# Quiet ends of the residuals and undisturbed reading of scores in a two-layer decoder trunk

## The chip, the cores and the metric

The kernel runs on one core of a Trainium2 chip. The metric is the device time of one execution in microseconds (us); a kernel's time is the median of its runs. The engines are TensorE (PE in the profile, PEld for its weight loads), VectorE (DVE), ScalarE (ACT), GpSimd (POOL) and SyncE (SP), which issues the transfers of the weights.

## The reference

One sequence of 256 tokens, width 1024, goes through two layers. Each layer has a half-step SwiGLU FFN, an attention, and another half-step FFN. Each of these sublayers is normalised first, shifted and scaled by vectors that are made from c, and gated by a third one:

```python
mod = silu(c) @ ada_w[layer] + ada_b[layer]
sh1, sc1, g1, sh2, sc2, g2, sh3, sc3, g3 = split(mod, 9)
h = rms_norm(x, norm_g[layer, 0]) * (1 + sc1) + sh1
x = x + 0.5 * g1 * swiglu(h, ffn_w_in[layer, 0], ffn_w_out[layer, 0])
h = rms_norm(x, norm_g[layer, 1]) * (1 + sc2) + sh2
x = x + g2 * mix        # layer 0: differential attention, layer 1: forgetting attention
h = rms_norm(x, norm_g[layer, 2]) * (1 + sc3) + sh3
x = x + 0.5 * g3 * swiglu(h, ffn_w_in[layer, 1], ffn_w_out[layer, 1])
```

In the differential attention each of 8 heads has two softmaxes over scores with a relative bias; the second, times lambda, is subtracted from the first, and the result multiplies v. All is in fp32.

## The kernel before, in words

**The matrices.** x lies transposed in SBUF, 8 tiles of 128 features by 256 tokens. Every product in fp32 is made of three matmuls on rounded halves (`mm3`): weight high times activation high, weight low times activation high, weight high times activation low. Weights come by SP in pieces of up to 128 x 1024 (`raw`, six buffers). ACT makes the high half of a piece (`wh`, a cast, `cp_part`), DVE the low half (`wl`, a subtraction, `sub_part`). For the normalised x the halves are `HH` and `HL`.

**The modulation.** The vectors sh, sc and g are made on DVE, out of the way of PE: one block (`ada`, 128 x 1024, `ada_block`, line 198) multiplies 128 rows of the weights by silu(c) and sums. Two blocks share a tile of 1 MB with three buffers; when the second one is done, its buffer is free and SP is told to load the next tile into it (`ada_dma`, line 185). There are 160 blocks. `need` (line 236) makes, at the place where it is called, all blocks that a modulation still lacks.

**What sets the order.** The program is written in one order, and a wrapper for each engine (`InOrder`, line 40) keeps a rough clock of its own for that engine. Casts, subtractions and ada blocks are background work: `bg` (line 386) issues them after each `mm3` where ACT's or DVE's clock is behind PE's; `fill_act` and `fill_dve` (lines 367 and 372) issue them ahead of an instruction whose operands are not ready by that clock. An ada block needs a credit, which grows with PE's work and is at most 6. `plain` and `plainly` run a function with the filling switched off. `take` (line 338) hands out the next weights of the stream and makes the halves that are still missing on the spot. `later` puts an operation off by some calls of `run_laters`.

**The residual.** `x_update` (line 438) adds gate times the product to one of the 8 tiles of x (DVE), writes the scaled tile's halves (HH on ACT, HL on DVE) and its square `sq` (ACT), and adds the squares up in `acc` (DVE behind an FFN, POOL behind an attention, the eighth always on DVE). The next sublayer starts on halves that are not normalised yet (`lp`, `lq`, or `lg` and `lu` of an FFN of kind "late"): PE runs its first steps, then the sum of `acc` over partitions (`psn`), from which `rstd_of` (line 460) makes the factor that is applied to the results. After its "late" first block an FFN goes on with halves that are normalised (`pg`, `pu`; `hid` is its hidden layer, `po` its output).

**The first attention.** A group for head t (line 1161) has the scores of head t, the transposed weights of t - 1, the values of t - 2, and the turned output of t - 3. `exps` (line 1084) reads the scores from PSUM on DVE in four instructions (`nl`, `nm`), each followed by an exponential on ACT. Groups 0 to 7 stand among the projections of v, q and k; 7 to 10 among the steps of the output projection (`pw`). Before the change, `exps` is plain in the group of the last head alone. `finish` (line 872) ends the output projection: it calls `need` for the attention's gate and for the scale and shift of the FFN behind it, which is 64 blocks from the start of the kernel, then updates x tile by tile.

**The start.** c is spread over all partitions by two matmuls (`pc`) of a row of ones with c in row 96 of a tile `crow`, whose other rows are zero; ACT makes silu(c) of it (`cact`). Before, between and behind, PE multiplies a constant tile (`warm`).

Of the kernel before, what the change touches and what calls it, by code (L numbers as in the profile page):

```python
# [10 lines left out]
F32 = mybir.dt.float32  # L11
F32R = mybir.dt.float32r
BF16 = mybir.dt.bfloat16
AF = mybir.ActivationFunctionType
ALU = mybir.AluOpType
PSUM = bass.MemoryType.PSUM

P = 128
D = 1024
S = 256  # L20
NC = D // P
HD = 64
AH = 8
# [17 lines left out]
CP_FIT = 0.9  # L41
DVE_FIT = 0.6
# [62 lines left out]
def trunk(ctx, tc, a, out):  # L105
# [3 lines left out]
    act = InOrder(tc, nc.scalar, 0.13, 1 / 1200)  # L109
    dve = InOrder(tc, nc.vector, 0.08, 1 / 960)  # L110
# [5 lines left out]
    kp = ctx.enter_context(tc.tile_pool(name="kp", bufs=2))  # L116
# [8 lines left out]
    def abank(name):  # L125
        return pp.tile([P, 512], F32, tag="ta", name=name)
# [6 lines left out]
    def plain(f, *args):  # L133

        r = []
        act.plainly(lambda: dve.plainly(lambda: r.append(f(*args))))
        return r[0]

    crow = ap_.tile([P, 2, D], F32, tag="ada", name="crow").rearrange("p a b -> p (a b)")
# [6 lines left out]
    ones = cp_.tile([P, P], F32, name="ones")  # L146
    first_in = []
    dve.memset(ones, 1.0 / D)
    dve.memset(crow[96:97, D:D + P], 1.0)
    dve.memset(crow[:96, :D + P], 0.0)  # L150
    eps = cp_.tile([P, 1], F32, name="eps")
    dve.memset(eps, EPS)
    half = cp_.tile([P, 2], F32, name="half")
# [136 lines left out]
    credit = [0.0]  # L290
    pace = [0.0]
    mode = ["hold"]
    laters = []

    def w_dma(count=NRAW):
# [65 lines left out]
    def work(cols):  # L361

        credit[0] = min(CREDIT, credit[0] + pace[0] * 2 * cols / 2048)
        if mode[0] != "hold":
            bg()

    def fill_act(start):
        while (mode[0] != "hold" and act.t + CP_FIT < start
               and len(his) < min(len(pieces), len(raws), done[0] + NHI)):
            cp_part()  # L370

    def fill_dve(start):

        while mode[0] != "hold" and dve.t + DVE_FIT < start:
            full = len(los) - begun[0]
            if mode[0] == "run" and credit[0] >= 1.0 and (full >= FULL or not splittable()):
                credit[0] -= 1.0
                dve.plainly(ada_block)
            elif splittable():
                sub_part()  # L380
            else:
                break
# [30 lines left out]
    def flush():  # L413
        for e in laters[:]:
            laters.remove(e)
            e[1]()

    def mm3(ps, w, xx, first, last):
        (wh, wl), (xh, xl) = w, xx
        mm(ps, wh, xh, start=first, stop=False, skip_group_check=True)  # L420
        mm(ps, wl, xh, start=False, stop=False, skip_group_check=True)
        mm(ps, wh, xl, start=False, stop=last, skip_group_check=True)
        work(P)
# [14 lines left out]
    def x_update(n, ps, gate, nxt, acc_eng):  # L438

        dve.scalar_tensor_tensor(x[n], ps, gate[:, n:n + 1], x[n], op0=ALU.mult, op1=ALU.add)
        hh, hl = hn[n]
        A = mods[nxt[0]][1]
        act.activation(hh, x[n], AF.Copy, scale=A[:, n:n + 1])
        sq = kp.tile([P, S], F32, tag="sq", name=f"sq{n}")
        act.activation(sq, x[n], AF.Square)

        def second():
            dve.scalar_tensor_tensor(hl, x[n], A[:, n:n + 1], hh.bitcast(F32),  # L450
                                     op0=ALU.mult, op1=ALU.subtract)
            if n == 0:
                acc[0] = sq
            else:
                t = kp.tile([P, S], F32, tag="acc", name="acc", bufs=1) if n == 1 else acc[0]
                (acc_eng if n < NC - 1 else dve).tensor_tensor(t, acc[0], sq, op=ALU.add)
                acc[0] = t
        return second

    def rstd_of(then=None, parts=None):  # L460
# [106 lines left out]
    def ffn(l, i, kind, m, nxt, at=2):  # L567
# [130 lines left out]
        for n in range(NC):  # L698
            po = mmbank(f"po{n}")[:, :S]
            if n == NC - NFILL:  # L700
                mode[0] = "fill"
            for hf in range(2):
                blk = take("wout")
                if n == NC - 1 and hf:
                    need(*nxt)
                    shift_cols(nxt)
                for kk in range(11):
                    k = hf * 11 + kk
                    if n == 0 and k == 18:
                        flush()  # L710
                        flush()
                    hh, hl = hid[k // 2]
                    o = (k % 2) * 256
                    mm3(po, blk(kk * P), (hh[:, o:o + 256], hl[:, o:o + 256]), k == 0, k == 21)
                    if kk in (1, 4, 6, 9):
                        run_laters()
            need(gate)
            if n >= 4:
                need(nxt[0])

            def upd(n=n, po=po):
                f = x_update(n, po, mods[gate][1], nxt, dve)
                if (l, i) == (0, 0) and n < NC - 1:
                    late["spread"](n)
                later(1, f)
            if n < NC - 1:
                later(1, upd)
            else:
                flush()
                flush()  # L730
                upd()
                flush()

    class Last:

# [194 lines left out]
    def warm(n):  # L930

        pw = bbank("warm")
        for _ in range(n):
            mm(pw[:, :P], ones, ones, start=True, stop=True)
# [21 lines left out]
    pc = [sbank(f"pc{i}") for i in range(2)]  # L956
    for i in range(2):
        mm(pc[i], crow[:97, D:D + P], crow[:97, i * 512:(i + 1) * 512], start=True, stop=True)
    psn = abank("psn")
    for k in range(0, NC, 2):  # L960
        sq = kp.tile([P, 512], F32, tag="w512a" if k % 4 else "w512b", name=f"sqs{k}")
        xk = xx[:, k:k + 2].rearrange("p a b -> p (a b)")
        if k == 2:
            dve.tensor_tensor(sq, xk, xk, op=ALU.mult)
        else:
            act.activation(sq, xk, AF.Square)
        sq4.append(sq)
        if k % 4:
            i = k // 4
            act.activation(cact[:, i * 512:(i + 1) * 512], pc[i], AF.Silu)  # L970
            sq = sq4[2 * i]
            dve.tensor_tensor(sq, sq, sq4[2 * i + 1], op=ALU.add)
            dve.tensor_tensor(sq[:, :S], sq[:, :S], sq[:, S:], op=ALU.add)
            warm(4 - 3 * i)
            for t in range(2):
                mm(psn[:, t:t + 1], sq[:, t * P:t * P + P], ones[:, :1], start=i + t == 0, stop=i == 1,
                   skip_group_check=True)
# [72 lines left out]
    def attention_a():  # L1050
# [33 lines left out]
        def exps(hd, sb):  # L1084
            g = gs[hd]
            nl = []
            nm = kp.tile([P, 4], F32, tag="nm", name=f"nm{hd}")
            sm = kp.tile([P, 4], F32, tag="sm", name=f"sm{hd}")
            for m in range(2):
                s = sb[m]  # L1090
                n_ = cp_.tile([P, 384], F32, tag=f"hidh{4 + 2 * (hd % 2) + m}", name=f"nl{hd}_{m}")
                nl.append(n_)
                for qt, (c0, w) in enumerate(QT):
                    cc = 2 * m + qt
                    dve.tensor_tensor_reduce(
                        n_[:, c0:c0 + w], s[:, c0:c0 + w], g[:, S - w:], -0.125, BIG,
                        ALU.add, ALU.min, accum_out=nm[:, cc:cc + 1])
                    act.activation(n_[:, c0:c0 + w], n_[:, c0:c0 + w], AF.Exp,
                                   bias=nm[:, cc:cc + 1], scale=-1.0,
                                   accum_out=sm[:, cc:cc + 1])  # L1100
            st[hd], sms[hd] = nl, sm
# [59 lines left out]
        def group(t):  # L1161

            hs, hw, hv, ho = (h if 0 <= h < AH else None for h in (t, t - 1, t - 2, t - 3))
            bank = bbank(f"po{t}") if hv is not None or ho is not None else None
            sb = scores(hs) if hs is not None else None
            pw = weights_t(hw) if hw is not None else None
            if hv is not None:
                values(hv, bank[:, :256])
            if ho is not None:
                out_t(ho, bank[:, 256:])  # L1170
            if hw is not None:
                wt = cp_.tile([P, 384], F32, tag=f"hidh{8 + hw % 2}", name=f"wt{hw}")
                act.copy(wt, pw[:, :384])
                st[hw] = wt
            if hs is not None:
                plain(exps, hs, sb) if hs == AH - 1 else exps(hs, sb)
            if hv is not None:
                squares(hv, bank[:, :256])
                inv_rms(hv)
            if ho is not None:  # L1180
                plain(out_split, ho, bank[:, 256:]) if ho == AH - 1 else out_split(ho, bank[:, 256:])
# [398 lines left out]
```

## Time and profile before

| what | before |
|---|---|
| median of 3 runs, us | 966.03 (965.13 to 966.9) |
| the profiled execution's own time, us | 964.94 |
| its span, us | 962.9 |
| instructions | 20487 |
| mean granted TensorE clock | 0.998 |
| moved by the transfers | 267.89 MB, mean 278 GB/s |

The prediction quotes rows of several views. A row of the timeline has start and duration in us from the span's start, the engine, the operation as out<-in with its shape, how many in a row it stands for, and in brackets the idle time of the engine ahead of it with what ended it. A row of the chain has start, duration, engine and tile. A row of the waits has who waited for whom, the total in us, how often, and the longest. A row of the windows has a stretch, its length, each engine's busy time with the count of its instructions, then TensorE's granted clock, the share of the DMA engines and GB/s. Names are those of the kernel without numbers; most instructions carry line 100, the wrapper's, so they are told by tile.

### The profile page before, as it was taken

How to read it: one execution, taken by the hardware profiler on the slowest of the kernel's cores; microseconds unless marked ns; L12 is line 12 of the kernel's file. 1: busy time of each engine (PE TensorE's matmuls, PEld its weight loads, DVE VectorE, ACT ScalarE, POOL GpSimd, SP SyncE). 2: the span in 40 equal slices, each digit the busy share in tenths (PEclk: the TensorE clock that was granted, in tenths of full speed). 3: DMA queues.
4: the chain of work that ended last, by engine and by line, in shares of the span. 5: the costliest groups of instructions: out<-in, count | busy, mean ns of one | idle time of the engine just before them, and what ended most of it. 6: DMA issues, size and time to landing. Idle time of an engine off the chain costs nothing.

```text
span 962.9 us, 20487 instructions
## 1 busy us (share of the span) xinstructions
PE 954.6 (99%) x8090; PEld 930.9 (97%) x8090; DVE 821.1 (85%) x1369; ACT 556.9 (58%) x908; POOL 72.5 (8%) x119
## 2 busy tenths in 40 slices
PE   9999999999999999999999999999999999999997
PEld 7999999988999999999997999999998899999997
DVE  8989988889999999878889988889988799555575
ACT  6575655566777645455577554445568766554432
POOL 0000001100112000000000000000044014200000
PEclk9999999999999999999999999999999999999999
DMA  9998989968767699878959899988995437987641
GB/s 369 413 368 311 376 314 317 372 216 292 280 214 255 211 389 375 293 280 315 330 198 369 303 340 339 343 294 317 317 323 163 118 128 219 268 166 253 192 148 44
DMA packets 69661, 267.89 MB, mean 278 GB/s; under 512 B 9572, under 2 KB 10413, under 8 KB 59454
## 3 DMA queue, kind: packets, MB, share of 16 engines
q1 hardware_dynamic: 66060, 259.35, 76.7%
q0 software_dynamic: 3072, 6.92, 2.5%
q8 instruction: 63, 1.03, 0.4%
q10 hardware_dynamic: 434, 0.33, 0.1%
q14 instruction: 32, 0.26, 0.1%
HBM read 264.42 MB, written 2.66 MB: 277 GB/s over the span
## 4 chain that ended last, share of the span: by engine, by line
PE 92%; DVE 4%; ACT 2%; issue 2%; DMA 0%; POOL 0%; SPq 0%; DVEq 0%; ACTq 0%; POOLq 0%
PE po L100 25%; PE pg L100 22%; PE pu L100 21%; PE pv L100 5%; PE pf L100 5%; PE lp L100 4%; PE pw L100 3%; DVE wl L100 1%; PE lq L100 1%; PE lu L100 1%; PE lg L100 1%; PE pk L100 1%; DVE nl L100 1%; PE wb L100 1%; ACT nl L100 1%
## 5 line engine op out<-in xcount | busy, mean ns | idle before, releaser
L100 ACT CAST wh<-raw 128x1024 fp32r<-128x1024 f32 (+1 forms) x360 | 347.8, 975 | 212.2 <-PE pu L100 87.2
L100 DVE TENSOR_TENSOR wl<-raw,wh 128x1024 fp32r<-128x1024 f32 (+1 forms) x360 | 400.1, 1126 | 76.1 <-ACT sg L100 25.0
L100 DVE CUSTOM_DVE_ANT_0 ada<-ada,cact,vecs 128x1024 f32<-128x1024 f32 x144 | 182.6, 1277 | 0.0
L100 PE MATMUL pg<-HH,wl 128*128 128x256 f32 x608 | 167.9, 276 | 0.0
L100 PE MATMUL pu<-HH,wh 128*128 128x256 f32 x608 | 167.9, 276 | 0.0
L100 PE MATMUL pg<-HH,wh 128*128 128x256 f32 x608 | 167.9, 276 | 0.0
L100 PE MATMUL pu<-HL,wh 128*128 128x256 f32 x608 | 167.9, 276 | 0.0
L100 PE MATMUL pg<-HL,wh 128*128 128x256 f32 x608 | 167.9, 276 | 0.0
L100 PE MATMUL pu<-HH,wl 128*128 128x256 f32 x608 | 167.9, 276 | 0.0
L100 PE MATMUL po<-hidh,wh 128*128 128x256 f32 x528 | 145.7, 276 | 0.0
L100 PE MATMUL po<-hidh,wl 128*128 128x256 f32 x528 | 145.7, 276 | 0.0
L100 PE MATMUL po<-hidl,wh 128*128 128x256 f32 x528 | 145.7, 276 | 0.0
L100 PEld LDWEIGHTS pg<-HH,wl 128*128 128x128 f32 x608 | 114.1, 188 | 0.0
L100 PEld LDWEIGHTS pg<-HH,wh 128*128 128x128 f32 x608 | 114.1, 188 | 0.0
L100 PEld LDWEIGHTS pg<-HL,wh 128*128 128x128 f32 x608 | 114.2, 188 | 0.0
L100 PEld LDWEIGHTS pu<-HH,wh 128*128 128x128 f32 x608 | 114.2, 188 | 0.0
L100 PEld LDWEIGHTS pu<-HL,wh 128*128 128x128 f32 x608 | 114.1, 188 | 0.0
L100 PEld LDWEIGHTS pu<-HH,wl 128*128 128x128 f32 x608 | 114.1, 188 | 0.0
L100 PEld LDWEIGHTS po<-hidl,wh 128*128 128x128 f32 x528 | 99.1, 188 | 0.0
L100 PEld LDWEIGHTS po<-hidh,wl 128*128 128x128 f32 x528 | 99.1, 188 | 0.0
L100 PEld LDWEIGHTS po<-hidh,wh 128*128 128x128 f32 x528 | 99.1, 188 | 0.0
L100 ACT CAST hidh<-hf 128x512 fp32r<-128x512 f32 x44 | 27.3, 621 | 45.4 <-DVE hf L100 45.4
(244 smaller groups left out, 1878.0 us busy)
## 6 DMA issues: line engine op xcount, KB each, us to landing
raw<-in_win SPq DMA_DIRECT2D x176, 512.0 KB, 5.8
ada<-in_ada SPq DMA_DIRECT2D x79, 1024.0 KB, 7.3
raw<-in_wout SPq DMA_DIRECT2D x48, 384.0 KB, 5.5
raw<-in_wout SPq DMA_DIRECT2D x48, 320.0 KB, 5.2
raw<-in_wqk SPq DMA_DIRECT2D x16, 512.0 KB, 5.2
raw<-in_wo SPq DMA_DIRECT2D x16, 512.0 KB, 5.2
raw<-in_wlast SPq DMA_DIRECT2D x16, 512.0 KB, 4.3
raw<-in_wv SPq DMA_DIRECT2D x8, 512.0 KB, 9.0
```

The lines of the kernel that those rows point to most:

```text
L100: return self.tc.keep_in_program_order(f(*args, **kw))
```

## The change

In the program's order of work four things change. While a flag `quiet` is set, no background work is issued; it is set in the last of the 8 output tiles of an FFN, after step 3 of its second half, and cleared when that tile of x is updated. In the last tile of any residual, `sq` is made ahead of HH, and `acc` ahead of HL. In the first attention `exps` is plain in all groups. At the start the large memset of `crow` stands ahead of the small one, one `warm` stands between the two matmuls that spread c, and two behind them are gone (four are three, one is none).

```diff
@@ start
     dve.memset(ones, 1.0 / D)
+    dve.memset(crow[:96, :D + P], 0.0)
     dve.memset(crow[96:97, D:D + P], 1.0)
-    dve.memset(crow[:96, :D + P], 0.0)
@@ work, fill_act, fill_dve
-        if mode[0] != "hold":
+        if mode[0] != "hold" and not quiet[0]:
             bg()
-        while (mode[0] != "hold" and act.t + CP_FIT < start
+        while (not quiet[0] and mode[0] != "hold" and act.t + CP_FIT < start
-        while mode[0] != "hold" and dve.t + DVE_FIT < start:
+        while not quiet[0] and mode[0] != "hold" and dve.t + DVE_FIT < start:
@@ x_update
+        sq = kp.tile([P, S], F32, tag="sq", name=f"sq{n}")
+        if n == NC - 1:
+            act.activation(sq, x[n], AF.Square)
         act.activation(hh, x[n], AF.Copy, scale=A[:, n:n + 1])
-        sq = kp.tile([P, S], F32, tag="sq", name=f"sq{n}")
-        act.activation(sq, x[n], AF.Square)
-
-        def second():
+        if n < NC - 1:
+            act.activation(sq, x[n], AF.Square)
+
+        def low():
             dve.scalar_tensor_tensor(hl, x[n], A[:, n:n + 1], hh.bitcast(F32),
                                      op0=ALU.mult, op1=ALU.subtract)
+
+        def second():
+            if n < NC - 1:
+                low()
...
                 (acc_eng if n < NC - 1 else dve).tensor_tensor(t, acc[0], sq, op=ALU.add)
                 acc[0] = t
+            if n == NC - 1:
+                low()
@@ ffn, output tiles
                     mm3(po, blk(kk * P), (hh[:, o:o + 256], hl[:, o:o + 256]), k == 0, k == 21)
+                    if n == NC - 1 and hf and kk == 3:
+                        quiet[0] = True
...
                 upd()
                 flush()
+                quiet[0] = False
@@ spread of c
         mm(pc[i], crow[:97, D:D + P], crow[:97, i * 512:(i + 1) * 512], start=True, stop=True)
+        warm(1 - i)
...
-            warm(4 - 3 * i)
+            if not i:
+                warm(3)
@@ group of the first attention
-                plain(exps, hs, sb) if hs == AH - 1 else exps(hs, sb)
+                plain(exps, hs, sb)
```

PE's order is the same but for the `warm` matmuls. On DVE, background work moves. The first place is the fifth head's group in the first attention, on DVE: `wl` is background subtractions, `nl` and `nm` the readings of the scores, `ada` a modulation block, `ss` the start of the norm of another head. Before:

```order
L100 TENSOR_TENSOR wl_3319<-raw_3018,wh_3206 128x1024
L100 ISA nl4_0_3351,nm4_3349<-s4_0_3332,g4_3169 128x128
L100 TENSOR_TENSOR wl_3354<-raw_3037,wh_3297 128x1024
L100 ISA nl4_0_3351,nm4_3349<-s4_0_3332,g4_3169 128x256
L100 ISA nl4_1_3360,nm4_3349<-s4_1_3333,g4_3169 128x128
L100 ISA nl4_1_3360,nm4_3349<-s4_1_3333,g4_3169 128x256
L100 ISA ada_3064,modall_91<-ada_3064,cact_89,vecs_75 128x1024
L100 TENSOR_SCALAR ss2_3366<-ss2_3366 128x2
```

The same place after:

```order
L100 TENSOR_TENSOR wl_3307<-raw_3015,wh_3202 128x1024
L100 ISA nl4_0_3342,nm4_3340<-s4_0_3323,g4_3165 128x128
L100 ISA nl4_0_3342,nm4_3340<-s4_0_3323,g4_3165 128x256
L100 ISA nl4_1_3347,nm4_3340<-s4_1_3324,g4_3165 128x128
L100 ISA nl4_1_3347,nm4_3340<-s4_1_3324,g4_3165 128x256
L100 TENSOR_TENSOR wl_3356<-raw_3031,wh_3285 128x1024
L100 TENSOR_SCALAR ss2_3353<-ss2_3353 128x2
```

The second subtraction moved behind the readings, and the ada block is gone from the group. (Each `nl` row and each `ada` row has a short one behind it that reads the sum; it is left out here.) Ahead of the last head's combine there were 59 ada blocks on DVE, now there are 52.

The second place is the finish of the first attention's output projection, on DVE: `ol` is the last head's low half, `HL` with `modall` the shift, `x` the residual's updates from `pw`. Before:

```order
L100 SCALAR_TENSOR_TENSOR ol3_2603<-po10_3896,small_90,oh3_2599 128x256
L100 ISA ada_3483,modall_91<-ada_3483,cact_89,vecs_75 128x1024
L100 TENSOR_TENSOR HL_93<-modall_91,HH_92 128x8x2
L100 SCALAR_TENSOR_TENSOR x_76<-pw0_3644,modall_91,x_76 128x256
L100 TENSOR_TENSOR wl_3934<-raw_3659,wh_3863 128x1024
L100 SCALAR_TENSOR_TENSOR x_76<-pw1_3645,modall_91,x_76 128x256
L100 SCALAR_TENSOR_TENSOR HL_93<-x_76,modall_91,HH_92 128x256
```

The same place after, where each of the four `ada` rows stands twice in a row:

```order
L100 SCALAR_TENSOR_TENSOR ol3_2597<-po10_3882,small_90,oh3_2593 128x256
L100 ISA ada_3073,modall_91<-ada_3073,cact_89,vecs_75 128x1024
L100 ISA ada_3810,modall_91<-ada_3810,cact_89,vecs_75 128x1024
L100 ISA ada_3837,modall_91<-ada_3837,cact_89,vecs_75 128x1024
L100 ISA ada_3890,modall_91<-ada_3890,cact_89,vecs_75 128x1024
L100 TENSOR_TENSOR HL_93<-modall_91,HH_92 128x8x2
L100 SCALAR_TENSOR_TENSOR x_76<-pw0_3630,modall_91,x_76 128x256
L100 SCALAR_TENSOR_TENSOR x_76<-pw1_3631,modall_91,x_76 128x256
L100 SCALAR_TENSOR_TENSOR HL_93<-x_76,modall_91,HH_92 128x256
```

One block before the updates has become eight, and the subtraction between the first two updates is gone from there. The third place is a little further on, on DVE after the change: the end of the same residual.

```order
L100 TENSOR_TENSOR acc_3962<-acc_3962,sq7_4022 128x256
L100 SCALAR_TENSOR_TENSOR HL_93<-x_76,modall_91,HH_92 128x256
L100 TENSOR_TENSOR wl_4033<-raw_3645,wh_3849 128x1024
L100 TENSOR_TENSOR wl_4070<-raw_3688,wh_3919 128x1024
L100 TENSOR_TENSOR wl_4080<-raw_3748,wh_4064 128x1024
L100 SCALAR_TENSOR_TENSOR ra_4092<-psn_4087,eps_83,r0_4089 128x256
```

The first of the three subtractions, `wl_4033`, is the one that stood between the updates (`wl_3934`); on PE its first reader is the second matmul of step 3 of 8 of `lg`, ahead of `psn`, before and after alike.

More of the change, by code (lines that the diff above doesn't have):

```diff
@@ L292, in trunk @@
     mode = ["hold"]
+    quiet = [False]
     laters = []
```

## The prediction

> **What bounds the kernel now.** I read the page's busy line first, then who TensorE (PE) waited for.
>
> ```profile
> PE 954.6 (99%) x8090; PEld 930.9 (97%) x8090; DVE 821.1 (85%) x1369; ACT 556.9 (58%) x908; POOL 72.5 (8%) x119
> PE warm L100 <- DVE ones L100: 1.1, 1, 1.1
> PE pf L100 <- DVE wl L100: 0.2, 1, 0.2
> PE s L100 <- ACT qk L100: 0.2, 1, 0.2
> ```
>
> The last three rows are all the waits of PE over the whole span: 1.5 us. A busy PE could still be a slow one, since matmuls overlap, so I looked at spacing in the chain of waits and at the end of the first residual.
>
> ```profile
> 133.47 59.84 PE po L100 x528
> 193.31 2.89 PE lp L100 x24
> 196.21 0.43 PE psn L100 x2
> 193.35 0.48 DVE L100 SCALAR_TENSOR_TENSOR x<-po,modall,x 128x256 f32<-128x256 f32 x1 [0.53 <-PE po L100]
> 194.81 0.42 DVE L100 TENSOR_TENSOR acc<-acc,sq 128x256 f32<-128x256 f32 x1
> ```
>
> 59.84/528 = 0.1133 us per matmul, and lp follows po with no gap (133.47 + 59.84 = 193.31). VectorE (DVE) already waited 0.53 us for the last po before its update of x, and the sum acc was done at 195.23, 1.0 us before psn, its reader. So there is no PE wait at a residual's end, and PE sets the pace from about 13 us to the last matmul. A change can then gain little; it loses whatever it makes PE wait. The question is who comes late anywhere after it. The next three windows are the first attention up to its last group, its end, and the output projection's residual.
>
> ```profile
> core 0: us, PE busy (x) PEld busy (x) DVE busy (x) ACT busy (x) POOL busy (x), PEclk, DMA share, GB/s
> 230.00:285.40 55.40, 55.20 (x480) 52.36 (x479) 51.57 (x135) 41.64 (x123) 6.99 (x11) 1.00 0.75 264
> 285.40:295.20 9.80, 9.75 (x86) 9.55 (x85) 9.49 (x18) 6.16 (x15) 0.94 (x2) 1.00 0.98 362
> 295.20:305.20 10.00, 10.00 (x87) 10.00 (x86) 9.70 (x20) 8.79 (x19) 4.81 (x6) 1.00 0.60 216
> ```
>
> DVE is 93% busy in the groups, 97% behind them: there is next to no room for work put off to the end.
>
> **The change part by part.** The start: memsets of crow in the other order, one warm-up between the two spreads of c.
>
> ```profile
> 2.68 3.78 PE L100 MATMUL pc<-crow 97*128 97x512 f32 x4
> 5.82 1.15 ACT L100 ACTIVATE sqs<-x 128x512 f32<-128x512 f32 x2 [0.20 <-DMA x<-in_x]
> 6.88 0.57 ACT L100 ACTIVATE cact<-pc 128x512 f32<-128x512 f32 x1
> 7.00 0.69 DVE L100 TENSOR_TENSOR sqs<-sqs,sqs 128x512 f32<-128x512 f32 x1 [0.54 <-ACT sqs L100]
> ```
>
> The spread is over at 6.46, its reader starts at 6.88 after squares that waited for x until 5.82. Those squares hide it: 0 us; without that cover the added warm-up, some 0.4 us. I take 0, with 0.4 either way.
>
> The quiet blocks (casts and subtractions held back in the last wout block until x is updated) and sq and acc drawn ahead: acc comes earlier, but psn already has it 1.0 us early. 0 at the three residuals of the FFNs. One subtraction moves behind acc there; it feeds the second pair of weights, half a projection later.
>
> The scores: in every group nothing may stand between the four readings of the scores. In the order, 59 blocks of the modulation (ada) stood on DVE ahead of the last combine, now 52. The output projection's finish needs 64, so 12 instead of 5 come between that combine and the residual: 4 where 4 were, and 8 in a row where 1 was. The rows of that place:
>
> ```profile
> 283.99 0.28 ACT L100 ACTIVATE on<-po 128x128 f32<-128x128 f32 x1 [0.41 <-PE po L100]
> 284.71 0.17 DVE L100 TENSOR_SCALAR ss<-ss 128x2 f32<-128x2 f32 x1
> 285.41 1.28 DVE L100 CUSTOM_DVE_ANT_0 ada<-ada,cact,vecs 128x1024 f32<-128x1024 f32 x1
> 293.60 1.27 DVE L100 CUSTOM_DVE_ANT_0 ada<-ada,cact,vecs 128x1024 f32<-128x1024 f32 x1
> 294.80 0.08 DVE L100 DVE_READ_ACCUMULATOR2_ANT modall<- 128x1 f32 x1
> 295.25 0.48 DVE L100 SCALAR_TENSOR_TENSOR x<-pw,modall,x 128x256 f32<-128x256 f32 x1
> 295.64 1.22 DVE L100 TENSOR_TENSOR wl<-raw,wh 128x1024 fp32r<-128x1024 f32 x1
> 304.04 0.41 DVE L100 TENSOR_TENSOR acc<-acc,sq 128x256 f32<-128x256 f32 x1
> 304.37 3.48 DVE L100 TENSOR_TENSOR wl<-raw,wh 128x1024 fp32r<-128x1024 f32 x3
> ```
>
> DVE cannot use the time it gains in the groups to come earlier to this place: ss waits for squares on ScalarE (ACT), and those waited for PE at 283.99. So the four blocks start at 285.4 as before, the eight at 293.6. A block costs 294.80 - 293.60 = 1.20 us; seven more are 8.4, and x's first update moves from 295.25 to 303.7.
>
> The blocks come in pairs with three buffers: the transfer for the last pair is issued when the first pair of the eight is done, at 293.6 + 2.4 = 296.0.
>
> ```profile
> L100 SPq DMA_DIRECT2D ada<-in_ada x3: 327/328/328, 286.7 to 294.9; - x3
> DMA to landing us min/median/max: 6.4/6.5/7.1
> ```
>
> It lands 6.5 us later, at 302.5, where the last two blocks were due at 300.8; they end at 304.9, and the first update starts at about 305.4 (call it T). Bounds: 303.7 without a wait, 306.0 with 7.1.
>
> Then the residual itself, 8.8 us from 295.25 to acc. Of this the 1.13 us of wl between the first two updates goes, but the sum on GpSimd (POOL) paces the rest:
>
> ```profile
> 299.56 4.27 POOL L456 TENSOR_TENSOR acc<-acc,sq 128x256 f32<-128x256 f32 x5 [0.53 <-ACT sq L100]
> 295.97 0.51 ACT L100 ACTIVATE HH<-x,modall 128x256 fp32r<-128x256 f32 x1
> 300.83 0.28 PE L100 MATMUL lg<-HH,wh 128*128 128x258 f32 x1
> 303.83 0.28 PE L100 MATMUL lg<-HH,wl 128*128 128x258 f32 x1
> 312.82 0.28 PE L100 MATMUL pg<-HH,wh 128*128 128x256 f32 x1
> ```
>
> Five sums take 4.27 and end at 303.83, just ahead of acc. Between all of the 1.13 gained and none I take 0.5: acc at T + 8.3, the last HL (now behind it) until T + 9.0, then the first wl, 3.48/3 = 1.16, until T + 10.2. That wl is the one which used to stand at 295.64, and the row at 303.83 is its first reader: the second matmul of the third of eight steps of lg. Behind it, on PE's own queue, stands everything else, psn included. PE goes on at 305.4 + 10.2 = 315.6 instead of 303.83: **11.8 us**. Bounds 9.5 (no wait for the transfer, all 1.13 gained) and 12.9. Next late could be the normalised HH and HL for pg, read from 312.82 + 11.8 = 324.6 on; ra follows the three wl, here at 307.85 with 5.0 us to pg, then at T + 12.4 = 317.8 with 6.8 us: not late. Nothing later gives the time back, since PE waits nowhere else.
>
> PE's pauses: it starts lg when the first HH is written, T + 1.2 = 306.6 (296.48 in the row above, 1.2 behind the update), instead of at 300.83, and does two steps (24 matmuls, 2.9 us), then waits from 309.5 to 315.6: 5.5 and 5.8 us without a matmul. What that does to its clock shows only at the two ends of this run:
>
> ```profile
> 6.00:7.00 1.00, 1.00 (x5) 0.75 (x4) 0.43 (x2) 1.00 (x3) 0.00 (x0) 1.00 1.02 418
> 7.00:8.00 1.00, 1.00 (x10) 1.00 (x9) 0.96 (x2) 0.98 (x2) 0.00 (x0) 1.00 1.03 422
> 956.00:958.00 2.00, 0.21 (x2) 0.01 (x1) 1.64 (x7) 0.79 (x2) 0.00 (x0) 1.00 0.35 120
> 959.00:960.00 1.00, 0.00 (x0) 0.00 (x0) 0.00 (x0) 0.00 (x0) 0.00 (x0) 0.88 0.38 151
> 960.00:963.00 3.00, 0.00 (x0) 0.00 (x0) 0.00 (x0) 0.00 (x0) 0.00 (x0) 0.50 0.32 124
> ```
>
> The last matmul ends at 956.21; 0.88 in the window to 960 and 0.50 behind it put the fall to half at 959.76, 3.5 us later. Both pauses are longer. PE had its first matmul at 1.1 and doubled its rate near 7 (5 a us, then 10): about 6 us at half. At half clock at most half the time is lost, 3 us; bounds 0 (no fall) and 3.3. I take 2.4, below the top since here PE recovers on gapless work.
> [...]
>
> Sum: 11.8 + 2.4 = 14.2 on the profiled execution's 964.94 us is 979.1. The median of the three runs is 966.03, 1.1 above it, so 980.2.
>
> **The rivals.**
> *No fall of the clock.* [...] 966.03 + 11.8 = 977.8. For it: the only fall seen came after 3.5 us, and the two pauses are not far above. 24%.
> *No change.* The eight blocks are hidden, because DVE arrives 8.4 us earlier than I say, the time it no longer works in the groups. It would need ss of the next-to-last groups free of PE; the row at 283.99 speaks against it. Or PE's lead hides them: between x at 295.25 and lg at 300.83 lie 5.6 us, of which HH takes 1.2; the 4.4 us of lead that are left do not cover 10. Then 966.0. 7%.
> *Faster.* ACT and DVE slow PE's reads in the attention.
>
> ```profile
> 292.51 8.48 PE pw L100 x72
> ```
>
> 8.48/72 = 0.1178 against 0.1133. If quieter groups brought all 480 matmuls of the window from 230 to 285.4 to 0.1133, that is 2.2 us: 963.8. It decides only if the pause above stays under 2.2 us, so the blocks would have to be hidden as well. 5%.
> My forecast, pause and fall: 64%.
>
> **How the numbers follow.** Likeliest 980.2. Its bounds: 966.03 + 9.5 + 0 = 975.5 and 966.03 + 12.9 + 3.3 = 982.2; with the runs' scatter of 0.9 either way 974.6 to 983.1, which holds the first rival too and 88% in all. A measurement of this kernel can tell about 0.2% (1.9 us) from no change. Slower by more: 64 + 24 = 88%; within: 7%; faster: 5%.
>
> **What would show it.** In the changed profile: eight ada blocks in a row on DVE from about 293.6, with a short wait for a transfer before the last two; x's first update at 305; POOL's acc later by as much; PE waiting for DVE twice, near 301 and 310, over 10 us in all where it waited 0.2; PEclk at 0.5 for some us behind 315; everything else up to 285 and behind 330 in step with before. Wrong if PE has no wait over 2 us near 301 to 316, if the four blocks start well ahead of 285, or if the residuals of the FFNs show a new PE wait.

## The result, and the profile after

The changed kernel takes 978.24 us (median of 6 runs, 975.9 to 981.06) against 965.62 for the kernel before, timed beside it (6 runs): a ratio of 1.012, 95% interval 1.0104 to 1.0136. The forecast was slower, 980.2 within 974.6 to 983.1. Its profiled execution took 978.14 us, with a span of 976.3 where before it was 962.9.

The busy line first, from the page, and all the waits of PE:

```profile
PE 958.3 (98%) x8088; PEld 934.9 (96%) x8088; DVE 822.5 (84%) x1369; ACT 557.4 (57%) x908; POOL 73.8 (8%) x119
PE pw L100 <- DVE x L100: 7.2, 1, 7.2
PE lg L100 <- DVE wl L100: 1.9, 1, 1.9
PE warm L100 <- DVE ones L100: 1.1, 1, 1.1
PE psn L100 <- DVE sqs L100: 1.1, 1, 1.1
```

Two waits for DVE are new at the first attention's end, 9.1 us together, and one of 1.1 at the start. The same three windows as before, and two behind them:

```profile
core 0: us, PE busy (x) PEld busy (x) DVE busy (x) ACT busy (x) POOL busy (x), PEclk, DMA share, GB/s
230.00:285.40 55.40, 55.40 (x480) 52.47 (x479) 43.83 (x120) 41.61 (x124) 6.57 (x10) 1.00 0.62 203
285.40:295.20 9.80, 9.80 (x86) 9.69 (x85) 9.52 (x17) 6.27 (x15) 1.38 (x2) 1.00 0.84 309
295.20:305.20 10.00, 3.76 (x32) 3.56 (x31) 9.05 (x16) 0.00 (x0) 0.00 (x0) 0.86 1.01 397
305.20:316.00 10.80, 7.91 (x52) 7.71 (x53) 9.30 (x22) 9.78 (x21) 4.76 (x6) 0.81 0.35 128
316.00:325.00 9.00, 9.00 (x62) 8.81 (x62) 7.19 (x12) 3.97 (x6) 0.00 (x0) 0.81 0.61 186
```

In the groups DVE has 7.7 us less to do (43.83 for 51.57), and PE does the same 480 matmuls in the window: DVE's ease brings PE no more of them. Behind the groups the loss comes: from 295.2 to 305.2 PE is busy for 3.76 us while DVE works on. DVE's own rows there:

```profile
285.51 0.17 DVE L100 TENSOR_SCALAR ss<-ss 128x2 f32<-128x2 f32 x1 [0.22 <-ACT on L100]
286.21 1.28 DVE L100 CUSTOM_DVE_ANT_0 ada<-ada,cact,vecs 128x1024 f32<-128x1024 f32 x1
...
294.36 1.27 DVE L100 CUSTOM_DVE_ANT_0 ada<-ada,cact,vecs 128x1024 f32<-128x1024 f32 x1
...
302.59 1.28 DVE L100 CUSTOM_DVE_ANT_0 ada<-ada,cact,vecs 128x1024 f32<-128x1024 f32 x1 [0.92 <-DMA ada<-in_ada]
...
305.64 0.87 DVE L100 SCALAR_TENSOR_TENSOR x<-pw,modall,x 128x256 f32<-128x256 f32 x2
...
313.60 0.42 DVE L100 TENSOR_TENSOR acc<-acc,sq 128x256 f32<-128x256 f32 x1 [0.63 <-POOL acc L464]
313.94 0.48 DVE L100 SCALAR_TENSOR_TENSOR HL<-x,modall,HH 128x256 fp32r<-128x256 f32 x1
314.34 3.49 DVE L100 TENSOR_TENSOR wl<-raw,wh 128x1024 fp32r<-128x1024 f32 x3
```

ss waits for ACT, as the forecast had it, so the blocks cannot begin earlier: the four start at 286.21, 0.80 us later than before, where ss is later by as much. Eight stand in a row from 294.36, with a wait for a transfer ahead of the seventh; x is first updated at 305.64 and not at 295.25. On PE:

```profile
298.69 0.28 PE L100 MATMUL pw<-ol,wh 128*128 128x256 f32 x1
306.18 0.58 PE L100 MATMUL pw<-oh,wh 128*128 128x256 f32 x1 [7.21 <-DVE x L100]
...
310.47 0.28 PE L100 MATMUL lg<-HH,wh 128*128 128x258 f32 x1
...
315.61 0.39 PE L100 MATMUL lg<-HH,wl 128*128 128x258 f32 x1 [1.91 <-DVE wl L100]
```

PE stops earlier than forecast, still inside the output projection: its fifth output tile lies in the other half of the PSUM bank of the first (`self.banks[n % 4]`), and waits until the first update has read that one (305.64 and 0.48 for the first of the two updates in that row, 306.12; PE goes on at 306.18). The second stop is the one at the third step of lg, and it ends at 315.61.

### The profile page after: what moved, and what is told of

Its sections match the earlier page's. It is cut to its first block, busy times and chain, and to the rows that moved or that the text cites. A ratio compares the mean times of both kernels' runs of the same rounds, so it can differ in the third digit from the quotient of the medians.

```text
span 976.3 us, 20496 instructions
## 1 busy us (share of the span) xinstructions
PE 958.3 (98%) x8088; PEld 934.9 (96%) x8088; DVE 822.5 (84%) x1369; ACT 557.4 (57%) x908; POOL 73.8 (8%) x119
## 4 chain that ended last, share of the span: by engine, by line
PE 95%; DVE 2%; DMA 1%; ACT 1%; POOL 0%; issue 0%; SPq 0%; DVEq 0%; ACTq 0%
PE po L100 25%; PE pg L100 21%; PE pu L100 21%; PE pv L100 5%; PE pf L100 5%; PE lp L100 4%; PE pqk L100 3%; PE pw L100 3%; PE lq L100 1%; PE pk L100 1%; PE lg L100 1%; PE lu L100 1%; DVE ada L100 1%; PE wb L100 1%; PE sb L100 1%; PE s L100 1%
## 5 line engine op out<-in xcount | busy, mean ns | idle before, releaser
L100 PE MATMUL po<-wh,hidh 128*128 128x256 f32 x176 | 48.6, 276 | 0.0
```

The source lines that it names most:

```text
L100: return self.tc.keep_in_program_order(f(*args, **kw))
```

## The experiments

The names in the expectations: A is the forecast's mechanism (blocks piled up ahead of the updates), B the quiet ends with the sum drawn ahead, C the edited start. "Before" is the median of the kernel before beside each batch.

**1. Which edit?** Four kernels, beside 966.47 us for the kernel before. `scores_only` is the kernel before with one edit:

```diff
-                plain(exps, hs, sb) if hs == AH - 1 else exps(hs, sb)
+                plain(exps, hs, sb)
```

> The kernel before with one edit: the readings of the scores stand without background work in all groups. Theory A (the modulation blocks that pile up in the finish of the first attention make the loss): 9 blocks stand ahead of the first update there, so 10 to 13 us over the kernel before, 976 to 979; PE waits over 6 us in pw or lg near 300 to 316. Theory B (the quiet blocks and the end of the residual, which put a subtraction behind the sum, make it): within 2 us of the kernel before. Theory C (the edited start makes a part of it): here the start is that of before, so the first pf is at 12.1 and not at 13.6.

It took 979.38 us, ratio 1.0137 (1.0117 to 1.0156), 12.9 over the kernel before and 0.4 above the top of the range; PE waits 10.1 us in pw and 1.6 in lg, and the first pf is at 12.30. `all_but_scores` is the changed kernel with that line undone:

> The changed kernel with the scores read as before, so that one block stands ahead of the first update, as in the kernel before. Theory A: within 1.5 us of the kernel before, what is left being the start. Theory B: 10 us or more slower, with PE waiting for a subtraction near 304. Theory C: the first pf is 1 to 1.5 us later than before and the total by as much.

965.22 us, ratio 0.9992 (0.9982 to 1.0002), and PE has no wait above 0.3 us behind the start. So the whole loss, as far as these medians can tell, sits in the one line about the scores; B falls. `start_only` is the kernel before with the three edits of the start alone:

> The kernel before with the edited start alone. Theory C1 (one warm-up fewer behind the spreads leaves PE idle for 1.1 us ahead of the second half of the sum, and TensorE's clock falls for a window): 0.8 to 1.5 us slower, with granted clock 0.5 in a window between 6 and 15 and the first pf at 13 or later. Theory C2 (the fall in the changed kernel's profile hung on where the clock's windows lay in that run): 0 to 0.7 us slower in the median, and the profile may show either. As predicted at first: 0 within 0.4.

965.53 us, ratio 0.9992 (0.998 to 1.0004), first pf at 12.09: C1 falls as a cost of every run, C2 stands (more on the start below).

`blocks_back` keeps the calm readings and puts ten blocks behind them by hand:

```diff
                 plain(exps, hs, sb)
+                for _ in range((0, 1, 1, 1, 1, 2, 2, 2)[hs]):
+                    dve.plainly(ada_block)
```

> The changed kernel with its calm readings of the scores, but with 10 modulation blocks placed by hand behind the readings of groups 1 to 7 (1, 1, 1, 1, 2, 2, 2), so that again one block stands ahead of the first update. Theory A: the 10 to 12 us are gone, 965 to 967.5, and PE has no wait over 1 us from 230 to 330. Rival (the calm readings themselves, or the quiet ends, cost): 5 us or more slower than before. If the calm readings help PE, as the rival of the prediction had it, it is up to 2 us faster than all_but_scores.

966.81 us, ratio 1.0004 (0.9993 to 1.0015): the loss is gone with the pile, though the readings stay calm. No gain from the calm shows in the time either; from its waits of PE:

```profile
PE pw L100 <- DVE wl L100: 1.6, 1, 1.6
...
PE psn L100 <- DVE sqs L100: 1.1, 1, 1.1
```

The blocks now push a subtraction back, and PE waits for it once, 1.6 us until 284.27, where no wait over 1 us was expected; with that it is no better than before.

**2. How does the pile cost it?** Four more, beside 966.72. `pile_only` leaves the readings of the kernel before, filled with subtractions, but keeps `fill_dve` from putting a block into a group:

```diff
+                no_ada[0] = True
                 plain(exps, hs, sb) if hs == AH - 1 else exps(hs, sb)
...
                 inv_rms(hv)
+            no_ada[0] = False
@@ fill_dve
-            if mode[0] == "run" and credit[0] >= 1.0 and (full >= FULL or not splittable()):
+            if mode[0] == "run" and not no_ada[0] and credit[0] >= 1.0 and (full >= FULL or not splittable()):
```

> The kernel before with its readings of the scores filled by subtractions as before, but no modulation block allowed in a group of the first attention, so that 9 blocks stand ahead of the first update (as in scores_only). Theory A: 976 to 980, like scores_only. If it is the calm reading that costs: within 2 us of the kernel before.

978.17 us, ratio 1.0118 (1.0102 to 1.0134), PE waits 9.2 and 1.3 us. Nine blocks stand ahead of the first update, as in `scores_only`. With uncalm readings and a pile the loss is back: it is the pile. `half_pile` is the changed kernel with one block behind the readings of groups 1 to 7, so that four stand ahead of the update:

> The changed kernel with one modulation block placed behind the readings of each of groups 1 to 7, so that 4 blocks and not 8 stand ahead of the first update. Theory A, by the terms of the prediction: the first update 3 blocks or 3.6 us later than before and no wait for a transfer, the subtraction that PE waits for done 10 us behind it, near 309.9 instead of 303.8; 6 us, with 0 to 2 for the clock: 971.5 to 974. If each block costs the same, 3 of 7 blocks are 5.4 us, 971. If PE's lead hides a pile of this size: 965 to 967.

Its first update on DVE, and the rows of PE that waited:

```profile
299.46 0.87 DVE L100 SCALAR_TENSOR_TENSOR x<-pw,modall,x 128x256 f32<-128x256 f32 x2
```

```profile
300.00 0.38 PE L100 MATMUL pw<-oh,wh 128*128 128x256 f32 x1 [1.48 <-DVE x L100]
304.60 0.39 PE L100 MATMUL lg<-HH,wh 128*128 128x258 f32 x1 [0.57 <-DVE x L100]
309.43 0.39 PE L100 MATMUL lg<-HH,wl 128*128 128x258 f32 x1 [1.89 <-DVE wl L100]
```

970.26 us, ratio 1.0035 (1.0004 to 1.0066). These rows of DVE and PE came where they were put, the first update at 299.46 and the subtraction's reader at 309.43 (expected 309.9), and its span, 968.6, is 5.7 above that of before; but no clock fell (granted clock 0.999 in the mean), and the median is 1.2 under the range given and only 3.5 above the kernel before, whose own runs went up to 972.33 in this batch. PE's lead does not hide even three blocks more: the three waits in these rows add up to 3.94 us. `wl_first` is the changed kernel with the subtraction back between the first two updates:

```diff
                 g = x_update(n, self.out(n), mods[gate][0], nxt, nc.gpsimd)
+                if n == 0 and gate == (0, 5):
+                    sub_part()
```

> The changed kernel with one edit: the subtraction that PE waits for in lg stands between the first two updates of x again, as in the kernel before; the eight blocks stay. If the late subtraction costs what the trace shows, PE's wait of 1.9 us in lg and the second fall of the clock (1.7 us) go and PE's first wait of 7.2 us stays: 974 to 975.5. If the sum behind it then ends last (acc is up to 1.1 us later), 976.5 to 977.5. If the eight blocks alone set the end: 978, as now.

978.04 us, ratio 1.0131 (1.0103 to 1.0159): no gain, where two of the three answers had one. Its waits of PE:

```profile
PE pw L100 <- DVE x L100: 7.4, 1, 7.4
...
PE pg L100 <- DVE wl L100: 0.9, 1, 0.9
...
PE lg L100 <- DVE wl L100: 0.2, 1, 0.2
```

The wait of 1.9 in lg is gone (the 0.2 stands at a later step), but 0.9 comes back in pg for a later subtraction. Behind its first wait PE worked at half rate in this run: its matmuls are 0.21 us apart from 307.29 to 310.49 and 0.12 from 310.70 on, and no long wait in lg stood behind that any more. That this half rate now counts, where a second wait swallowed it before, fits these rows; how the loss divides between it, the wait in pg and the sum is not shown.

**3. What does the clock cost?** `kept_busy` adds matmuls of the constant tile where PE would stand (at the fifth tile in `finish`, and ahead of the third step of lg); `idle(n)` multiplies the constant tile n times and leaves the wrapper's clock as it was:

```diff
+                if n == 4 and gate == (0, 5):
+                    idle(50)
...
+                    if k == 2 and l == 0:
+                        idle(24)
```

> The changed kernel with work added that leaves the result as it is: 50 matmuls of a constant tile ahead of the output projection's fifth tile in the finish, 24 ahead of the third step of lg, where PE would stand. If the clock's fall costs what the trace shows, granted clock is 1.00 from 295 to 325, PE still gets its subtraction near 315.5, and the time falls by 1.7 us or a little more, to 976 to 977. If the fall costs nothing, as the first rival had it: 978 or later.

982.02 us, ratio 1.0156 (1.014 to 1.0171). This settled nothing: one such product stands as two matmuls in the trace and took 0.22 us (the 50 ran from 298.13 to 309.21), so the 50 and 24 kept PE past both waits. With 33 and 14, beside the changed kernel once more and 966.49 for the kernel before:

> As kept_busy, with 33 and 14 multiplications of the constant tile in place of 50 and 24, since one took 0.227 us there and not the 0.13 counted on, so that PE was kept past both waits. They now end just before x's first update and before the subtraction. If the clock's fall is a cost of its own: granted clock 1.00 from 295 to 325, the second matmul of the third step of lg 10 us behind the first update as in the changed kernel, and the time 0.5 to 2 us below after_again. If the fall is hidden by the wait for DVE: within 0.5 us of after_again.

> The changed kernel unaltered, timed on the same chip as kept_busy2, with a second profile. Theory A: 976 to 980; PE waits over 6 us in pw and 1 to 2.5 in lg; the fall of the clock behind the second wait hangs on where the windows lie, so what is lost behind it is between 0.3 and 1.7 us.

977.79 us, ratio 1.0121 (1.0101 to 1.0141), and 977.11, ratio 1.0105 (1.0088 to 1.0122), for the changed kernel. In `kept_busy2` the granted clock is 1.00 from 297.50 to 319.00, and there is no gain; but the 14 still ended 1 us too late. In the second profile of the changed kernel PE waits 7.8 us in pw and 0.8 in lg, less than the 1 to 2.5 expected. Then 9 were tried, again beside the changed kernel and 965.17 for the kernel before:

> As kept_busy2, with 9 and not 14 multiplications at the second place, since those 14 ended 1 us behind the subtraction. Now PE is busy throughout and nothing is added to its path. If the fall of the clock costs what after's profile shows behind its second wait, 976 to 977, with the second matmul of the third step of lg 10 us behind x's first update and granted clock 1.00; if the fall is hidden by the wait for DVE in most runs, as after_again's profile shows, 977 to 978.

> The changed kernel unaltered once more, beside kept_busy3 on the same chip: 976 to 979, so that the two can be compared over some runs each.

978.61 us, ratio 1.0139 (1.012 to 1.0159), and 976.37, ratio 1.0115 (1.0095 to 1.0135), for the changed kernel. Keeping the clock up does not help, within what these runs can tell; the time even came above both ranges expected. In the profile of kept_busy3 the wait for the transfer was 2.80 us, the longest of all, where after_third's was 1.69; less these 1.11 us the two profiled times agree within 0.1 (977.71 and 976.65). DVE's first update and PE's second matmul of the third step of lg in kept_busy3:

```profile
306.17 0.87 DVE L100 SCALAR_TENSOR_TENSOR x<-pw,modall,x 128x256 f32<-128x256 f32 x2
316.14 0.38 PE L100 MATMUL lg<-HH,wl 128*128 128x258 f32 x1
```

They are 9.97 us apart at full clock (0.999 in the mean of this profile), and 9.97 in the profile of after (305.64 and 315.61), where the clock was 0.50 from 302.48 to 309.31, ahead of the second wait: that fall costs nothing. The windows of after_third, the changed kernel, show why:

```profile
306.25:309.67 3.42, 3.42 (x18) 3.42 (x18) 2.94 (x7) 2.94 (x9) 1.53 (x2) 0.50 0.71 290
309.67:313.08 3.41, 3.41 (x30) 3.41 (x30) 2.90 (x7) 2.98 (x9) 3.12 (x4) 1.00 0.01 2
313.08:316.49 3.41, 1.82 (x15) 1.62 (x14) 3.29 (x5) 2.88 (x4) 0.09 (x1) 1.00 0.14 13
316.49:319.91 3.42, 3.42 (x29) 3.37 (x28) 2.97 (x6) 1.93 (x3) 0.00 (x0) 1.00 0.84 284
```

PE works through the rest of pw at half rate, 18 matmuls in a window, and then waits for the subtraction all the same, 1.59 us within the third row: at full rate it would only have waited longer.

## Why the prediction was right, and where its sizes were off

**The start, 0 within 0.4.** Right in the median (`start_only`), but not in this profile, where the first pf comes at 13.61 for 12.07 and the first matmul of po 1.25 us later than before (134.72 for 133.47). ss is only 0.80 later, because between the two the profile of before took 0.45 longer (more under the rivals). The window from 5.52 to 8.93, in which PE waits 1.1 us for the sum of squares, is followed by one at half clock:

```profile
5.52:8.93 3.41, 2.33 (x17) 1.90 (x16) 2.80 (x5) 3.18 (x5) 0.00 (x0) 1.00 1.03 419
8.93:12.35 3.42, 3.42 (x18) 3.39 (x18) 2.39 (x8) 1.70 (x3) 0.00 (x0) 0.50 1.04 406
```

It was so in the profile of blocks_back too: PE waits 1.1 us for the sum, has 2.32 us of matmuls from 5.11 to 8.52, and the clock is 0.50 from 8.52 to 11.94. In that of `start_only` PE has no such wait, and the clock is 1.00 from 7.63 to 11.04. That the fall hung on where the clock's windows lay, as C2 has it, fits these three but is not shown by them.

**The quiet ends, 0.** Right: `all_but_scores` has them, and is the same as before. The end of the first FFN's residual in the changed kernel, on DVE:

```profile
194.60 0.48 DVE L100 SCALAR_TENSOR_TENSOR x<-po,modall,x 128x256 f32<-128x256 f32 x1 [1.97 <-PE po L100]
195.63 0.43 DVE L100 TENSOR_TENSOR acc<-acc,sq 128x256 f32<-128x256 f32 x1 [0.55 <-ACT sq L100]
```

and in the chain of waits

```profile
197.46 0.43 PE psn L100 x2
```

DVE now idles 1.97 us for the last po where it idled 0.53, and the sum is ready 1.4 us ahead of psn where it was 1.0: time won where nobody waited.

**The pile, 11.8.** Right in mechanism and in size. The times of five profiles, in us; the last column but one is PE's second matmul of the third step of lg:

| profile | ss | wait for the transfer | x's first update | lg | last matmul |
|---|---|---|---|---|---|
| before | 284.71 | none | 295.25 | 303.83 | 955.94 |
| after | 285.51 | 0.92 | 305.64 | 315.61 | 969.39 |
| after_again | 285.49 | 1.31 | 306.01 | 315.96 | 968.19 |
| after_third | 284.36 | 1.69 | 305.26 | 315.21 | 967.87 |
| kept_busy3 | 284.16 | 2.80 | 306.17 | 316.14 | 968.93 |

The wait for the transfer differs from run to run, and the first update moves by as much: from ss to the first update, less that wait, it is 19.21 us in each of the three profiles of the changed kernel and in kept_busy3 (305.64 - 285.51 - 0.92 in the first), for 10.54 before (295.25 - 284.71). The 8.7 us between are the seven blocks at 1.20 and 0.3. In the profile of after the transfer was issued at 296.87, as put but for the 0.80 of ss, and landed 5.7 us later where 6.5 was put: the wait was 0.92 and not 1.6. From the update to lg it took 9.97 us, put at 10.2. From ss to lg it is 19.12 us before and 30.10, 30.47 and 30.85 in the three, so the pile costs 10.98, 11.35 and 11.73 us, the last with a wait of the length that was put. That PE went on at 315.61 in the first of them, the number forecast, is in part luck: the pile was 0.8 smaller than the 11.8 put, and ss came 0.80 later.

**The first stop, put at lg near 301 and 5.5 us long.** Wrong in place: it was in pw, 7.2 us, and the second 1.9 instead of 5.8, because I followed the reads of HH and not the write into a bank that DVE had yet to read. (The forecast's own times give 306.6 - 300.83 = 5.8 and 315.6 - 309.5 = 6.1 for the two.) Together they were 9.1 us, where over 10 was put. It does not move the end, since DVE's chain sets 315.6 either way.

**The clock, 2.4.** This is the term that was mis-sized. The forecast took the 6 us of half rate at the kernel's start for what would follow the pauses, and put 2.4 of the 3 us lost by that on the path. No run shows that 2.4, nor its bound of 3.3, and that PE recovers sooner on gapless work was an estimate of mine. In the profile of after the clock did fall twice:

```profile
299.07:302.48 3.41, 0.00 (x0) 0.00 (x0) 2.60 (x6) 0.00 (x0) 0.00 (x0) 1.00 1.01 423
302.48:305.89 3.41, 0.00 (x0) 0.00 (x0) 3.00 (x7) 0.58 (x2) 0.00 (x0) 0.50 1.00 416
305.89:309.31 3.42, 3.13 (x14) 3.14 (x15) 3.02 (x8) 2.95 (x8) 0.82 (x2) 0.50 0.89 314
309.31:312.72 3.41, 3.41 (x31) 3.41 (x30) 3.21 (x8) 2.97 (x9) 3.14 (x4) 1.00 0.03 10
312.72:316.13 3.41, 1.50 (x13) 1.29 (x12) 2.78 (x5) 3.41 (x5) 0.81 (x1) 1.00 0.00 0
316.13:319.55 3.42, 3.42 (x16) 3.23 (x16) 1.89 (x3) 0.92 (x3) 0.00 (x0) 0.50 0.77 231
```

The first fall costs nothing, since PE waits again behind it. The second lasted 3.42 us, with PE busy throughout. It came in one of the changed kernel's three profiles; in its window PE does 16 matmuls, where 29 fit in the last window of after_third. From lg to the last matmul it is 652.11 us before and 653.78, 652.23 and 652.66 in the three: 1.67 more in the first, 0.12 and 0.55 in the two without a second fall. So that fall is worth some 1.1 to 1.6 us, and in the other two profiles nothing near 2.4 was lost. So the first rival, no fall on the path and 977.8, describes most runs better than the forecast did: over the 14 runs of the changed kernel the median is 977.1. For the profile of after the terms add up: the last matmul starts 13.45 us later than before, which is 0.80 up to ss, 10.98 of the pile and 1.67 behind lg, and the span grew by 13.4. The forecast of 980.2 was 2.0 above the median: 1.0 since 14.2 was put for the 13.2 that the profiled times differ by, and 1.0 for the 1.1 added from profile to median, of which the changed kernel showed 0.1.

**The rivals.** No change fell with PE's waits. Faster fell with `all_but_scores`: from the first matmul of po to ss it takes 150.79 us both with calm readings (285.51 - 134.72, the changed kernel) and without (284.88 - 134.09, all_but_scores). In the profile of before it took 151.24 (284.71 - 133.47), but `start_only`, with the same attention, took 150.89 (284.42 - 133.53), so that difference is not the readings'; that ACT and DVE slow PE's reads is shown by no run. The 2.2 us were also too much to hope for: they put the spacing of pw on the whole window, whose own row has 55.20 us for 480 matmuls, 0.1150 each, or 0.8 us. The chain's row of the changed kernel, the chain's and DVE's of all_but_scores:

```profile
134.72 59.84 PE po L100 x528
```

```profile
134.09 59.84 PE po L100 x528
```

```profile
284.88 0.17 DVE L100 TENSOR_SCALAR ss<-ss 128x2 f32<-128x2 f32 x1
```

No version was faster than the kernel before by more than its measurement can tell.

## What to carry to other kernels

Work that fills an engine's gaps is not free to be left out: if a later point demands a fixed amount of it, what is not done in the gaps is done there, in a row, ahead of the chain that everyone waits for; count the blocks ahead of that point before and after. When a pause and a second wait follow each other, price the clock only behind the last one: what runs slowly between them is swallowed by the second, as long as that wait does not end sooner (here 9.97 us from x's first update to lg, with half clock on the way and without). And look for the first thing that a stopped chain blocks: here it was a matmul that writes into a bank which another engine had yet to read (7.2 us), and not one that reads a late operand.

## What the runs showed of the hardware

In the profile of after TensorE's granted clock is 0.50 for 3.42 us (8.93 to 12.35), 6.83 us (302.48 to 309.31) and 3.42 us (316.13 to 319.55), and 1.00 between them. In after_again it is 0.50 for at least 10 us, in all of the stretch from 302.00 to 312.00. It came back to 1.00 behind the first wait at 309.31 in after and at 309.67 in after_third. The clock did not fall only behind stretches without a matmul: that from 312.72 to 316.13 in the profile of after has 1.50 us of matmuls in 3.41 (44%) and is followed by half rate. The stretch from 313.08 to 316.49 of after_third, shown above, has 1.82 (53%) and is followed by full rate, and so is this one of kept_busy3, with 1.68 (49%):

```profile
304.05:307.46 3.41, 1.68 (x15) 1.49 (x14) 2.71 (x9) 1.62 (x4) 0.00 (x0) 1.00 0.81 291
307.46:310.88 3.42, 3.25 (x23) 2.65 (x22) 3.21 (x8) 2.95 (x9) 1.78 (x3) 1.00 0.68 271
```

These rows give no border in PE's busy share: at the start of after, with matmuls of one column among them, a stretch with 2.33 us (68%) was followed by half rate too.
